# One pipeline of four phases over MoBA's eight heads, and two wide products first in keys and queries

## The chip, the cores and the metric

The kernel runs on one core of a Trainium2 chip. The metric is device microseconds of one execution. The changed kernel and the kernel before are timed on the same chip; differences under about 0.2% can't be told from none.

## The reference

One decoder layer on 256 tokens of width 1024, all in float32. A combined projection `x @ w_in` feeds two mixers: a gated linear recurrence (HGRN2) and a block attention (MoBA). With 256 tokens there is one block, so MoBA here is causal softmax attention over 8 heads of width 128, with rotary keys and queries. Both mixers are projected, gated, added and projected again, then come two layer norms and a SwiGLU network.

```python
proj = jnp.einsum('bsd,dn->bsn', x, w_in)
hq, hf, hi, hg, mq, mk, mv, gate_logits = jnp.split(proj, offsets, axis=-1)
y_a = rms_norm(hgrn2_mixer(...), ...) * jax.nn.silu(hg)
y_b = moba_attention(apply_rope(mq), apply_rope(mk), mv)
z_a = y_a @ w_branch_a; z_b = y_b @ w_branch_b
mixed = (g_a * z_a + g_b * z_b) @ w_out
x = layer_norm(DN_ALPHA * x + mixed, ln1_w, ln1_b)
y = (jax.nn.silu(h_gate) * h_up) @ w_ffn_down
return layer_norm(DN_ALPHA * x + y, ln2_w, ln2_b)
```

## The kernel before

Every large product is made of reduced-precision float32 (`fp32r`) parts: an operand is split into a high part (a cast on ScalarE, L192 or L220) and a low part (a subtraction on VectorE, L193 or L222), and TensorE adds high by high, high by low and low by high. The weights come as 77 tiles of 128 x 2048 in a fixed order (`plan`); `fetch` hands out the next pair `wh`, `wl` and keeps three more tiles being loaded, cast and subtracted ahead of it. There are three buffers for raw tiles and four for each of `wh` and `wl`, so a cast of tile i waits until TensorE has read tile i-4.

The change lies in the middle of the program. There the products with `w_in` for the attention are made: values `mv` (`values`, two halves of four heads), keys `mk` and queries `mq` (`rope_pair`, a pair of heads j each, j = 0 to 3), then the gate logits `ga` (`gates`), then the branch product `za`. `rope_pair` for j over 0 uses `wide_pair` (L324): for each k a product of 512 columns with `wh` (L335: x's high and low parts side by side) and one of 256 columns with `wl` (L337). Its argument `twos` says how many times, at the start of the tile's first half, two products with `wh` stand before two with `wl`.

Beside these products run the attention's heads (`moba_head`), as a generator that a list of side work (`Steps`) advances by one step after each `rope_pair` and after each half chunk of `values`, `gates` and `za`. A head has these parts:
- the split of its keys and queries into `kh`, `kl`, `qh`, `ql` on ScalarE and VectorE;
- the scores `s`: on TensorE one float32 product of 128 columns (L700, which the trace records as two matmuls) and three `fp32r` products (L705 to L707);
- the softmax in `ms` and `st`: VectorE adds the mask and takes maxima, ScalarE takes exponentials (L715, L716), VectorE scales by the reciprocals (L717 to L719);
- three transposes `pt` on TensorE (L723), copied out as `pTh`, `pTl` and `p1` (L727, L728);
- the product with the values, `po`, four matmuls (L731 to L734), split into `ybh`, `ybl`, which the branch product `zb` reads.

`moba_heads(h0, n)` runs four heads: a head's score part one step ahead of its transposes and its value product, which stand in the same step. Four heads are queued after keys and queries j = 1, the other four after j = 3, when the gate logits begin. ScalarE uses exponentials in the heads and sigmoids in the gate logits; to go from one to the other it loads a table (ACT_TABLE_LOAD).

The code's order gives only the dependences and a priority: in this part a scheduler sets each engine's order by its own timeline. Each engine then runs its list strictly in that order.

Of the kernel before, what the change touches and what calls it, by code (L numbers as in the profile page):

```python
# [11 lines left out]
F32R = mybir.dt.float32r  # L12
# [5 lines left out]
P = 128  # L18
T = 256
# [3 lines left out]
H = 8  # L23
# [15 lines left out]
HOLD_DOWN = 3  # L39
SUMS = 2  # L40
ORDERED = 2
DOWN = "SSPSTSTSPPP"
SUMS_AFTER = (8,12)
FAST = tuple(range(2, 2 + len(DOWN) - DOWN.count("P")))
PLAIN = tuple(q for q in range(NF // 2) if q not in FAST)
SEQUENCE = [PLAIN[DOWN[:i].count("P")] if s == "P" else FAST[i - DOWN[:i].count("P")] for i, s in enumerate(DOWN)]
AHEAD = [q for q, s in zip(SEQUENCE, DOWN) if s == "T"]

# [77 lines left out]
def hybrid_layer_kernel(ctx: ExitStack, tc, x, xw, vecs, bias, wts, ln1_w, ln1_b, ln2_w, ln2_b, consts, out):  # L126
# [7 lines left out]
    sm = pool("sm", 2)  # L134
    klp = pool("klp", 1)
    mm = pool("mm", 4, space=PSUM)
    aux = pool("aux", 4, space=PSUM)

    def slot(name, dt=F32):
        return big.tile([P, 2048], dt, tag="s8", name=name)  # L140

    def r32(ap):
        return ap.bitcast(F32)
# [47 lines left out]
    def split(dst_h, dst_l, src):  # L191
        nc.scalar.copy(dst_h, src)  # L192
        nc.vector.tensor_sub(dst_l, src, r32(dst_h))  # L193
# [84 lines left out]
    def fetch(ahead=LOOKAHEAD):  # L278
        while state["next"] < len(loads) and len(ready) < 1 + ahead:
            list(stage())  # L280
        return ready.pop(0)
# [6 lines left out]
    xp = Pair("xp")  # L288
# [27 lines left out]
    def feat_pair(name, ah=None, al=None):  # L316
        ah, al = (xTh, xTl) if ah is None else (ah, al)
        wh, wl = fetch()
        ps = mm.tile([P, 2, T], F32, tag="mm", name=name)
        for f in range(2):  # L320
            feat_steps(ps[:, f, :], wh, wl, f, ah, al, range(KC))
        return ps

    def wide_pair(name, a, p, tag, twos=0):  # L324


        wh, wl = fetch()
        pss = []
        for f in range(2):
            ps = p.tile([P, 2, T], F32, tag=tag, name=f"{name}{f}")  # L330
            wcol = slice(f * P, (f + 1) * P)
            n = twos if f == 0 else 0
            for ks in [(k, k + 1) for k in range(0, 2 * n, 2)] + [(k,) for k in range(2 * n, KC)]:
                for k in ks:
                    nc.tensor.matmul(ps, wh[:, k, wcol], a.both(k), start=(k == 0), stop=False)  # L335
                for k in ks:
                    nc.tensor.matmul(ps[:, 0, :], wl[:, k, wcol], a[0, k, slice(0, T)],  # L337
                                     start=False, stop=(k == KC - 1))
            pss.append(ps)
        return pss  # L340
# [114 lines left out]
    for j in range(4):  # L455
        sg = sm.tile([P, 2, T], F32, tag="sg", name=f"sgq{j}")
        sgs = [by_half(sg[:, f, :]) for f in range(2)]
        if j < HQ_WIDE:
            for f, ps in enumerate(wide_pair(f"hq{j}", xp, mm, "mm")):
                z = Qg[:, :, 2 * j + f, :]  # L460
# [7 lines left out]
        for f in range(2):  # L468
            h = 2 * j + f
# [156 lines left out]
    side = Steps()  # L626
# [17 lines left out]
    def values(c):  # L644
        cs = slice(c * 512, (c + 1) * 512)

        def evac(t, ps):
            if t == 0:
                split(mvh[:, cs], mvl[:, cs], ps)
            else:  # L650
                nc.scalar.copy(mv1[:, cs], ps)

        for _ in tok_chunk(f"mv{c}", evac):
            side.step()
# [21 lines left out]
    qT = slot("qT").rearrange("p (h t) -> p h t", h=H)  # L676
    kT = slot("kT").rearrange("p (h t) -> p h t", h=H)
# [3 lines left out]
    def rope_pair(nm, dst, j):  # L681
        if j == 0:
            ps = feat_pair(f"m{nm}{j}")
        else:
            ps = sm.tile([P, 2, T], F32, tag="sg", name=f"z{nm}{j}")
            for f, parts in enumerate(wide_pair(f"m{nm}{j}", xp, mm, "mm", {1: 1, 2: 2}.get(j, 0) if nm == "k" else 0)):
                nc.scalar.copy(ps[:, f, :], parts[:, 1, :])
                nc.vector.tensor_add(ps[:, f, :], parts[:, 0, :], ps[:, f, :])
        hs = slice(2 * j, 2 * j + 2)
        bc = lambda z: z[:, None, :].to_broadcast([P, 2, T])  # L690
        tmp = sm.tile([P, 2, T], F32, tag="sg", name=f"rt{nm}{j}")
        nc.scalar.copy(tmp[0:64], ps[64:P])
        nc.scalar.copy(tmp[64:P], ps[0:64])
        nc.vector.tensor_mul(dst[:, hs, :], ps, bc(cos))
        nc.gpsimd.tensor_mul(tmp, tmp, bc(sin))
        nc.gpsimd.tensor_add(dst[:, hs, :], dst[:, hs, :], tmp)

    def moba_head(h):
        ps = aux.tile([P, 3 * P], F32, tag="aux", name=f"s{h}")
        nc.tensor.matmul(ps[:, 0:P], qT[:, h, 0:P], kT[:, h, 0:P], start=True, stop=True)  # L700
        (kh, kl), (qh, ql) = [[sm.tile([P, n], F32R, tag=f"{tag}{z}", name=f"{nm}{z}{h}") for z in "hl"]
                              for nm, n, tag in (("k", T, "pT"), ("q", P, "q"))]
        split(kh, kl, kT[:, h, :])
        split(qh, ql, qT[:, h, P:T])
        nc.tensor.matmul(ps[:, P:3 * P], qh, kh, start=True, stop=False)  # L705
        nc.tensor.matmul(ps[:, P:3 * P], qh, kl, start=False, stop=False)
        nc.tensor.matmul(ps[:, P:3 * P], ql, kh, start=False, stop=True)  # L707
        s = sm.tile([P, 3 * P], F32, tag="ms", name=f"ms{h}")
        st = sm.tile([P, 8], F32, tag="st", name=f"st{h}")
        nc.vector.tensor_tensor(s, ps, causal, op=ALU.add)  # L710
        nc.vector.reduce_max(st[:, 0:1], s[:, 0:P], axis=mybir.AxisListType.X)
        nc.vector.reduce_max(st[:, 1:2], s[:, P:3 * P], axis=mybir.AxisListType.X)
        nc.vector.tensor_scalar(st[:, 2:4], st[:, 0:2], -SCALE, None, op0=ALU.mult)
        p = s
        nc.scalar.activation(p[:, 0:P], s[:, 0:P], AF.Exp, bias=st[:, 2:3], scale=SCALE, accum_out=st[:, 4:5])  # L715
        nc.scalar.activation(p[:, P:3 * P], s[:, P:3 * P], AF.Exp, bias=st[:, 3:4], scale=SCALE, accum_out=st[:, 5:6])  # L716
        nc.vector.reciprocal(st[:, 6:8], st[:, 4:6])  # L717
        nc.vector.tensor_scalar(p[:, 0:P], p[:, 0:P], st[:, 6:7], None, op0=ALU.mult)
        nc.vector.tensor_scalar(p[:, P:3 * P], p[:, P:3 * P], st[:, 7:8], None, op0=ALU.mult)  # L719
        yield  # L720
        pt = aux.tile([P, 3 * P], F32, tag="aux", name=f"pt{h}")
        for b in range(3):
            nc.tensor.transpose(pt[:, b * P:(b + 1) * P], p[:, b * P:(b + 1) * P], ident)  # L723
        pTh = sm.tile([P, T], F32R, tag="pTh", name=f"pTh{h}")
        pTl = sm.tile([P, T], F32R, tag="pTl", name=f"pTl{h}")
        p1 = sm.tile([P, P], F32, tag="pT", name=f"p1{h}")
        split(pTh, pTl, pt[:, 0:T])  # L727
        nc.scalar.copy(p1, pt[:, T:3 * P])  # L728
        hd = slice(h * P, (h + 1) * P)
        po = aux.tile([P, T], F32, tag="aux", name=f"po{h}")  # L730
        nc.tensor.matmul(po, mvh[:, hd], pTh, start=True, stop=False)  # L731
        nc.tensor.matmul(po, mvl[:, hd], pTh, start=False, stop=False)
        nc.tensor.matmul(po[:, P:T], mv1[:, hd], p1, start=False, stop=False)
        nc.tensor.matmul(po, mvh[:, hd], pTl, start=False, stop=True)  # L734
        split(ybh[:, h, :], ybl[:, h, :], po)
        yield

    def moba_heads(h0, n):
        heads = [moba_head(h) for h in range(h0, h0 + n)]
        next(heads[0])  # L740
        for i in range(n):
            if i < n - 1:
                next(heads[i + 1])
            next(heads[i])
            yield

    for c in range(2):
        if c == 1:
            values(1)
        for j in range(2 * c, 2 * c + 2):  # L750
            rope_pair("k", kT, j)
            side.step()
            rope_pair("q", qT, j)
            side.step()
        side.gens.append(moba_heads(4 * c, 4))
    ga = gates("ga", 0)


# [207 lines left out]

    for j in range(EARLY, NF - 2 * ORDERED, 2):
        ffn_step(j)

    with tc.manual_schedule(engines={ET.PE, ET.DVE, ET.Activation}):  # L970
        for j in range(NF - 2 * ORDERED, NF, 2):
            ffn_step(j)
# [54 lines left out]
        z, spare = [slot("z")[:, i:i + D] for i in (0, D)]  # L1027
# [8 lines left out]
        for i, (raw, (k0, wh, wl)) in enumerate(zip(last_raw, held)):  # L1036
# [5 lines left out]
            c = sums[:, 2 * i:2 * i + 2].unsqueeze(2).to_broadcast([P, 2, SUMS])  # L1042
# [106 lines left out]
```

## Time and profile before

| | |
|---|---|
| median of 3 runs | 492.94 us (492.85 to 493.57) |
| profiled execution: its time | 493.46 us |
| its span, first to last instruction | 491.7 us |
| mean granted TensorE clock | 0.998 |
| casts of weights on ScalarE (L220), 71 | 133.7 us busy, 1890 ns each |
| subtractions of weights on VectorE (L222), 71 | 162.4 us busy, 2293 ns each |

The span holds 1.8 us less than the time of the same execution. The page gives the busy time of each engine, the chain that ended last, and the groups of instructions; matmuls are pipelined, so one that is recorded with 389 ns lets the next start after some 230 ns. The distance between two starts is therefore what a matmul costs, and it is read from the timeline.

### The profile page before, as it was taken

The page shows a single profiled execution, that of the slowest core. Times are in us where ns is not written, and L with a number is a line of the kernel's source. Part 1 is how long each engine was busy: PE and PEld are TensorE (multiplying, and loading weights), DVE is VectorE, ACT ScalarE, POOL GpSimd, SP SyncE. Part 2 cuts the span into 40 slices and gives each one's busy share as a digit, 9 for nine tenths or more (in the row PEclk, how much of TensorE's full clock was granted, in tenths as well). Part 3 has the DMA queues.
Part 4 walks back from the last instruction along what each step waited for, and adds up shares of the span by engine and source line. Part 5 has one row for each costly group of instructions (what it writes and reads, how often), then busy time and mean ns, then how long its engine had stood idle before and what let it go on. Part 6 is the DMA issues. An engine that isn't in the chain of part 4 may idle for free.

```text
span 491.7 us, 6779 instructions
## 1 busy us (share of the span) xinstructions
PE 484.4 (99%) x2621; PEld 418.2 (85%) x2621; DVE 406.5 (83%) x523; ACT 297.5 (61%) x415; POOL 41.6 (8%) x46
## 2 busy tenths in 40 slices
PE   9999999999999999999999999999999999999994
PEld 9889888888899888888888888888888888888784
DVE  5879899999667998988765678856897878989996
ACT  6698587435756767777653462544655655576663
POOL 0000000000004441240000000000000000000030
PEclk9999999999999999999999999999999999999999
DMA  8977426644552346349544455247859644267852
GB/s 314 420 285 261 172 93 249 227 159 171 172 171 87 136 167 239 122 162 337 179 165 171 167 181 232 101 176 276 318 219 338 214 171 173 91 231 244 317 145 85
DMA packets 17631, 99.99 MB, mean 203 GB/s; under 512 B 1984, under 2 KB 3776, under 8 KB 7616
## 3 DMA queue, kind: packets, MB, share of 16 engines
q1 hardware_dynamic: 14400, 92.62, 51.9%
q0 software_dynamic: 3056, 6.82, 4.2%
q8 instruction: 20, 0.33, 0.3%
q10 hardware_dynamic: 144, 0.13, 0.1%
q14 instruction: 11, 0.09, 0.0%
HBM read 94.84 MB, written 3.15 MB: 199 GB/s over the span
## 4 chain that ended last, share of the span: by engine, by line
PE 90%; DVE 5%; issue 2%; ACT 1%; DMA 1%; DVEq 0%; POOLq 0%; POOL 0%; ACTq 0%
PE fu L335 7%; PE fg L335 7%; PE fg L337 3%; PE fu L337 3%; PE mk L335 2%; PE mq L335 2%; PE hq L335 2%; PE sc L542 2%; PE ga L387 1%; PE hf L360 1%; PE ga L388 1%; PE ga L386 1%; PE za L386 1%; PE za L387 1%; PE mv L386 1%
## 5 line engine op out<-in xcount | busy, mean ns | idle before, releaser
L222 DVE TENSOR_TENSOR wl<-raw,wh 128x2048 fp32r<-128x2048 f32 (+1 forms) x71 | 162.4, 2293 | 48.2 <-ACT wh L220 47.9
L220 ACT CAST wh<-raw 128x2048 fp32r<-128x2048 f32 (+1 forms) x71 | 133.7, 1890 | 62.2 <-PE fg L335 14.2
L335 PE MATMUL fg<-x1p,wh 128*128 128x512 f32 x144 | 50.5, 394 | 0.0
L335 PE MATMUL fu<-x1p,wh 128*128 128x512 f32 x144 | 50.4, 394 | 0.0
L337 PE MATMUL fg<-x1p,wl 128*128 128x256 f32 x144 | 40.0, 278 | 0.0
L337 PE MATMUL fu<-x1p,wl 128*128 128x256 f32 x144 | 39.9, 277 | 0.0
L335 PEld LDWEIGHTS fu<-x1p,wh 128*128 128x128 f32 x144 | 27.0, 187 | 6.2
L335 PEld LDWEIGHTS fg<-x1p,wh 128*128 128x128 f32 x144 | 27.0, 187 | 6.1
L337 PEld LDWEIGHTS fg<-x1p,wl 128*128 128x128 f32 x144 | 27.1, 188 | 0.1
L337 PEld LDWEIGHTS fu<-x1p,wl 128*128 128x128 f32 x144 | 27.1, 188 | 0.0
L335 PE MATMUL mq<-xp,wh 128*128 128x512 f32 x48 | 17.2, 396 | 0.0
L335 PE MATMUL mk<-xp,wh 128*128 128x512 f32 x48 | 17.0, 397 | 0.0
L589 POOL TENSOR_TENSOR ost<-ost,half 128x4 f32<-128x4 f32 x4 | 4.1, 1015 | 152.7 <-DVE ost L588 152.7
L335 PE MATMUL hq<-xp,wh 128*128 128x512 f32 x48 | 16.7, 394 | 0.0
L337 PE MATMUL mq<-xp,wl 128*128 128x256 f32 x48 | 13.5, 282 | 0.0
L337 PE MATMUL hq<-xp,wl 128*128 128x256 f32 x48 | 13.3, 277 | 0.0
L337 PE MATMUL mk<-xp,wl 128*128 128x256 f32 x48 | 13.1, 284 | 0.0
L388 PE MATMUL ga<-wl,xp 128*128 128x512 f32 x32 | 12.7, 398 | 0.0
L387 PE MATMUL za<-wh,yal 128*128 128x512 f32 x32 | 12.7, 397 | 0.0
L879 PE MATMUL fe<-wh,x1p 128*128 128x512 f32 x32 | 12.6, 395 | 0.0
L388 PE MATMUL gb<-wl,xp 128*128 128x512 f32 x32 | 12.6, 395 | 0.0
L805 PE MATMUL wo<-wh,mTh 128*128 128x512 f32 x32 | 12.6, 394 | 0.0
(379 smaller groups left out, 1367.9 us busy)
## 6 DMA issues: line engine op xcount, KB each, us to landing
raw<-in_wts_dram SPq DMA_DIRECT2D x69, 1024.0 KB, 4.8
rawcorners<-in_wts_dram SPq DMA_DIRECT2D x5, 1024.0 KB, 4.8
xw<-in_xw_dram SPq DMA_DIRECT2D x6, 640.0 KB, 8.8
rawahead<-in_wts_dram SPq DMA_DIRECT2D x2, 1024.0 KB, 4.9
rawsums<-spill SPq DMA_DIRECT2D x2, 1024.0 KB, 4.8
rawcorners<-in_wts_dram SPq DMA_DIRECT2D x2, 768.0 KB, 5.9
raw<-in_wts_dram SPq DMA_DIRECT2D x2, 512.0 KB, 11.8
xr<-in_x_dram POOLq DMA_DIRECT2D x1, 1024.0 KB, 5.4
```

The lines of the kernel that those rows point to most:

```text
L220: nc.scalar.copy(h[:, ks, :], raw[:, ks, :])
L222: eng.tensor_sub(l[:, ks, :], raw[:, ks, :], r32(h[:, ks, :]))
L335: nc.tensor.matmul(ps, wh[:, k, wcol], a.both(k), start=(k == 0), stop=False)
L337: nc.tensor.matmul(ps[:, 0, :], wl[:, k, wcol], a[0, k, slice(0, T)], start=False, stop=(k == KC - 1))
L360: nc.tensor.matmul(ps, wh[:, kk, wcol], xp.both(k), start=False, stop=False)
L386: nc.tensor.matmul(pss[t], ah[:, kk, ts], wh[:, k, :], start=(kk == 0), stop=False)
L387: nc.tensor.matmul(pss[t], al[:, kk, ts], wh[:, k, :], start=False, stop=False)
L388: nc.tensor.matmul(pss[t], ah[:, kk, ts], wl[:, k, :], start=False, stop=(kk == KC - 1))
L542: nc.tensor.matmul(ps[:, a, :], KL[:, h, :], later(Qt, n, h, 1), start=True, stop=True)
L589: nc.gpsimd.tensor_tensor(st[:, 8:12], st[:, 4:8], half, op=ALU.pow)
L805: nc.tensor.matmul(ps, lh(kk)[:, ts], wh[:, k, ns], start=(kk == first), stop=False)
L879: nc.tensor.matmul(ps, x1p[0, kk, ts], wh[:, k, :], start=(kk == 0), stop=False)
```

## The change

Four things are changed.

1. All eight heads form one pipeline, queued once, after keys and queries j = 1. A head begins at a step of its own (`STARTS`: 0, 1, 3, 5, 6, 7, 8, 9).
2. A head has four phases, at `LAGS` 0, 1, 3 and 5 steps after its beginning: the split of keys and queries; scores and softmax; transposes and their copies; the value product. In one step, older phases come first. The pipeline has 15 steps.
3. Keys' high and low parts lie in one tile `keys` of four slices (two heads), in the buffer that the recurrence used before, instead of two buffers each that they shared with the transposes' copies.
4. `twos` is 1 for all wide keys and for queries j = 2 and 3. Before it was 1 and 2 for keys j = 1 and 2 and 0 elsewhere.

```diff
+STARTS = (0, 1, 3, 5, 6, 7, 8, 9)
+LAGS = (0, 1, 3, 5)
...
-            for f, parts in enumerate(wide_pair(f"m{nm}{j}", xp, mm, "mm", {1: 1, 2: 2}.get(j, 0) if nm == "k" else 0)):
+            for f, parts in enumerate(wide_pair(f"m{nm}{j}", xp, mm, "mm", int(nm == "k" or j > 1))):
...
-    def moba_head(h):
+    def moba_head(h, keys):
+        kh, kl = [keys[:, 2 * (h % 2) + z, :] for z in range(2)]
+        qh, ql = [sm.tile([P, P], F32R, tag=f"q{z}", name=f"q{z}{h}") for z in "hl"]
+        split(kh, kl, kT[:, h, :])
+        split(qh, ql, qT[:, h, P:T])
+        yield
         ps = aux.tile([P, 3 * P], F32, tag="aux", name=f"s{h}")
         nc.tensor.matmul(ps[:, 0:P], qT[:, h, 0:P], kT[:, h, 0:P], start=True, stop=True)
-        (kh, kl), (qh, ql) = [[sm.tile([P, n], F32R, tag=f"{tag}{z}", name=f"{nm}{z}{h}") for z in "hl"]
-                              for nm, n, tag in (("k", T, "pT"), ("q", P, "q"))]
-        split(kh, kl, kT[:, h, :])
-        split(qh, ql, qT[:, h, P:T])
...
         nc.scalar.copy(p1, pt[:, T:3 * P])
+        yield
...
-    def moba_heads(h0, n):
-        heads = [moba_head(h) for h in range(h0, h0 + n)]
-        next(heads[0])
-        for i in range(n):
-            if i < n - 1:
-                next(heads[i + 1])
-            next(heads[i])
+    def moba_heads():
+        keys = klp.tile([P, 4, T], F32R, tag="kl", name="keys")
+        heads = [moba_head(h, keys) for h in range(H)]
+        for i in range(STARTS[-1] + LAGS[-1] + 1):
+            for lag in LAGS[::-1]:
+                for head, start in zip(heads, STARTS):
+                    if i == start + lag:
+                        next(head, None)
             yield
...
-        side.gens.append(moba_heads(4 * c, 4))
+        if c == 0:
+            side.gens.append(moba_heads())
```

What the scheduler makes of it is seen at three places. In these rows the changed kernel's line numbers are a few higher (L707 to L710 are the score products, L726 the transposes, L735 to L738 the value products), and the number behind a name's letters is the head.

On TensorE, in the first quarter of the branch product `za`, before:

```order
L731 MATMUL po4_2090<-pTh4_2084,mv_958 128x256
L732 MATMUL po4_2090<-pTh4_2084,mv_958 128x256
L700 MATMUL s6_2131<-kT_1319,qT_1318 128x128
L705 MATMUL s6_2131<-kh6_2133,qh6_2135 128x256
L723 MATMUL pt5_2155<-cst_89,ms5_2069 128x128
L706 MATMUL s6_2131<-kl6_2134,qh6_2135 128x256
L707 MATMUL s6_2131<-kh6_2133,ql6_2136 128x256
L723 MATMUL pt5_2155<-cst_89,ms5_2069 128x128 x2
```

and now:

```order
L726 MATMUL pt5_2207<-cst_89,ms5_2117 128x128 x3
L707 MATMUL s7_2217<-kT_1319,qT_1318 128x128
L708 MATMUL s7_2217<-keys_1596,qh7_2194 128x256
L709 MATMUL s7_2217<-keys_1596,qh7_2194 128x256
L710 MATMUL s7_2217<-keys_1596,ql7_2195 128x256
L735 MATMUL po4_2265<-pTh4_2172,mv_958 128x256
L736 MATMUL po4_2265<-pTh4_2172,mv_958 128x256
L737 MATMUL po4_2265<-p14_2174,mv1_959 128x128
L738 MATMUL po4_2265<-pTl4_2173,mv_958 128x256
L726 MATMUL pt6_2272<-cst_89,ms6_2183 128x128 x3
```

Parts of heads that lay among each other, with products of `za` between, are now whole and stand in a row; in the whole program the groups of float32 products of 128 columns on TensorE go from 51 to 43, with the same number of products in them. Between the transposes `pt4` and the transposes `pt5` there stand now the scores `s6`, the value product `po3` and 38 products of `za`.

On ScalarE, at the same time, before (`ga` rows are sigmoids, `ms` rows exponentials):

```order
L715 ACT_TABLE_LOAD
L715 ACTIVATE ms4_2045,st4_2046<-ms4_2045,st4_2046 128x128
L716 ACTIVATE ms4_2045,st4_2046<-ms4_2045,st4_2046 128x256
L220 CAST wh34_2246<-raw34_2245 128x2048
L715 ACTIVATE ms5_2069,st5_2070<-ms5_2069,st5_2070 128x128
L716 ACTIVATE ms5_2069,st5_2070<-ms5_2069,st5_2070 128x256
L667 ACT_TABLE_LOAD
L667 ACTIVATE ga_1999<-ga_1999 128x512
L192 CAST pTh4_2084<-pt4_2080 128x256
L192 CAST kh6_2133<-kT_1319 128x256
L220 CAST wh35_2299<-raw35_2298 128x2048
L667 ACTIVATE ga_1999<-ga_1999 128x512
```

and now, from the row behind the cast `wh35`:

```order
L669 ACT_TABLE_LOAD
L669 ACTIVATE ga_1935<-ga_1935 128x512
L718 ACT_TABLE_LOAD
L718 ACTIVATE ms5_2117,st5_2118<-ms5_2117,st5_2118 128x128
L719 ACTIVATE ms5_2117,st5_2118<-ms5_2117,st5_2118 128x256
L194 CAST pTh4_2172<-pt4_2168 128x256
L669 ACT_TABLE_LOAD
L669 ACTIVATE ga_1935<-ga_1935 128x512
L194 CAST ybh_1320<-po3_2200 128x256
L718 ACT_TABLE_LOAD
L718 ACTIVATE ms6_2183,st6_2184<-ms6_2183,st6_2184 128x128
L719 ACTIVATE ms6_2183,st6_2184<-ms6_2183,st6_2184 128x256
```

The two sigmoids of the last gate chunk stood together and now have the exponentials of head 5 between them: the program has two table loads more. The row behind the last one shown is the copy `p14` that `po4` above reads.

On ScalarE, while the queries j = 3 are made, now (`zk3` rows take keys j = 3 from PSUM, `rtq2` rows are the rotary halves of queries j = 2):

```order
L222 CAST wh30_1871<-raw30_1870 128x2048
L694 COPY rtq2_1770<-zq2_1725 64x512
L695 COPY rtq2_1770<-zq2_1725 64x512
L194 CAST pTh1_1847<-pt1_1843 128x256
L194 CAST keys_1596<-kT_1319 128x256
L194 CAST ybh_1320<-po0_1920 128x256
L689 COPY zk3_1792<-mk30_1799 128x256
L689 COPY zk3_1792<-mk31_1816 128x256
L718 ACTIVATE ms2_1858,st2_1859<-ms2_1858,st2_1859 128x128
L719 ACTIVATE ms2_1858,st2_1859<-ms2_1858,st2_1859 128x256
L731 COPY p11_1849<-pt1_1843 128x128
```

Before, the copy `p11` of head 1 came well ahead of the exponentials of head 2 (five rows ahead, with the weight cast `wh29` between them); now it stands behind them. The orders of SyncE, and of all engines before the values' second half and behind the first products of `zb`, are unchanged; on GpSimd one transfer has moved ahead of one rotary sum.

## The prediction

> **What bounds the kernel now.** I read the page first: busy time, clock, and the chain that ended last.
>
> ```profile
> span 491.7 us, 6779 instructions
> ...
> PE 484.4 (99%) x2621; PEld 418.2 (85%) x2621; DVE 406.5 (83%) x523; ACT 297.5 (61%) x415; POOL 41.6 (8%) x46
> ...
> PEclk9999999999999999999999999999999999999999
> ...
> PE 90%; DVE 5%; issue 2%; ACT 1%; DMA 1%; DVEq 0%; POOLq 0%; POOL 0%; ACTq 0%
> ```
>
> TensorE (PE) is busy for 484.4 of 491.7 us at full clock, and the chain runs 90% on it. A busy TensorE may still have idled between pipelined matmuls, so the second view is its waits, the whole list for that engine:
>
> ```profile
> PE warm L429 <- PEq L1136: 0.8, 1, 0.8
> ```
>
> It waits once, at the start. The third view is busy time by stretch (columns: length, then busy time and count for PE, weight loads, DVE, ACT, POOL), over the queries and keys, the gate logits, and the branch product `za`:
>
> ```profile
> 182.40:208.00 25.60, 25.60 (x158) 22.67 (x157) 21.93 (x44) 19.79 (x45) 6.83 (x6) 1.00 0.53 188
> 208.00:233.00 25.00, 25.00 (x124) 20.91 (x123) 21.02 (x35) 19.59 (x33) 7.18 (x7) 1.00 0.66 249
> 233.00:259.00 26.00, 26.00 (x133) 21.94 (x132) 18.45 (x32) 15.50 (x29) 0.00 (x0) 1.00 0.51 173
> ```
>
> TensorE fills every stretch that the change touches, while ScalarE has 5 to 10 us free in each. So this part ends when TensorE's list of matmuls ends. A new order gains only if the same matmuls cost less in it; it loses as soon as one of them comes due before its input is there.
>
> **The change, part by part.** *Gathered parts of heads.* No matmul is added or taken away; the float32 products of 128 columns lie in 43 groups instead of 51. What is a group's cost? Starts from the timeline, first three transposes in a row, then three that are parted by a product:
>
> ```profile
> 186.47 0.49 PE L723 MATMUL pt<-cst,ms 128*128 128x128 f32 x3
> 186.71 0.37 PE L337 MATMUL mk<-xp,wl 128*128 128x256 f32 x1
> 186.92 0.39 PE L335 MATMUL mk<-xp,wh 128*128 128x512 f32 x1
> ...
> 250.16 0.27 PE L723 MATMUL pt<-cst,ms 128*128 128x128 f32 x1
> 250.19 0.48 PE L386 MATMUL za<-wh,yah 128*128 128x512 f32 x1
> 250.50 0.38 PE L723 MATMUL pt<-cst,ms 128*128 128x128 f32 x2
> 250.64 0.48 PE L387 MATMUL za<-wh,yal 128*128 128x512 f32 x1
> 250.95 0.39 PE L388 MATMUL za<-wl,yah 128*128 128x512 f32 x1
> ```
>
> In a row: 186.47 to 186.92 is 0.45 us, less 0.12 for one 256-column product, 0.33. Parted: 250.16 to 250.95 is 0.79, less two 512-column products of 0.23, again 0.33. Each transpose costs 0.11 in either order. (The product behind a group seems 0.09 slow only because the group's starts are drawn together.) The score part agrees:
>
> ```profile
> 173.05 0.38 PE L700 MATMUL s<-kT,qT 128*128 128x128 f32 x2
> 173.18 0.37 PE L705 MATMUL s<-kh,qh 128*128 128x256 f32 x1
> 173.38 0.39 PE L386 MATMUL mv<-wh,xp 128*128 128x512 f32 x1
> ```
>
> 0.33 is two records of 0.11 and one product of 0.12. So gathering is worth 0.0 us. Bounds: if each group did cost 0.09 once, 8 fewer would gain 0.7; at the other end, nothing. I take 0, by the parted group, which is the direct comparison.
>
> *Two wide products first.* Keys j = 2 begins in that order, then alternates:
>
> ```profile
> 182.42 0.62 PE L335 MATMUL mk<-xp,wh 128*128 128x512 f32 x2
> ...
> 183.80 0.40 PE L335 MATMUL mk<-xp,wh 128*128 128x512 f32 x1
> ...
> 184.50 0.40 PE L335 MATMUL mk<-xp,wh 128*128 128x512 f32 x1
> ```
>
> Four pairs in 1.38 us, 0.345 each; two alternating pairs in 0.70, 0.35 each. The doubled beginnings go from 3 to 5: below 0.02 us. They give a late `wl` 0.23 us more, but TensorE never waited for one. 0.0.
>
> *ScalarE and VectorE.* Two table loads are added, the rest is moved. Here a cost appears only where TensorE is made to wait, so I work out the places where a matmul now stands soonest behind its input. The rows (for ScalarE then VectorE):
>
> ```profile
> 219.52 0.64 ACT L667 ACTIVATE ga<-ga 128x512 f32<-128x512 f32 x1
> 225.64 1.28 ACT L715 ACT_TABLE_LOAD   x1
> 226.93 0.40 ACT L715 ACTIVATE ms<-ms,st 128x128 f32<-128x128 f32 x1
> 227.73 0.19 ACT L716 ACTIVATION_READ_ACCUMULATOR ms<-ms,st 128x1 f32 x1
> 227.83 1.89 ACT L220 CAST wh<-raw 128x2048 fp32r<-128x2048 f32 x1
> 233.28 0.35 ACT L192 CAST pTh<-pt 128x256 fp32r<-128x256 f32 x1
> 241.81 0.26 ACT L728 COPY p<-pt 128x128 f32<-128x128 f32 x1
> ...
> 227.95 0.17 DVE L717 RECIPROCAL st<-st 128x2 f32<-128x2 f32 x1 [0.91 <-ACT ms L716]
> 228.35 0.35 DVE L719 TENSOR_SCALAR ms<-ms,st 128x256 f32<-128x256 f32 x1
> 229.75 2.29 DVE L222 TENSOR_TENSOR wl<-raw,wh 128x2048 fp32r<-128x2048 f32 x1 [1.05 <-ACT wh L220]
> 243.89 0.42 DVE L193 TENSOR_TENSOR ybl<-po,ybh 128x256 fp32r<-128x256 f32 x1
> ```
>
> A table load holds ScalarE for 1.29, a head's two exponentials for 0.90, reciprocal and scaling take 0.75. Two loads more are 2.6 us of ScalarE, covered by its idle time, unless a chain through them is due.
>
> Place A, first quarter of `za`. Let 0 be the end of the last `ga` product. TensorE: `pt4` 0.33, `s6` 0.57 (0.22 and three of 0.12), 38 products of `za` 8.76, `po3` 0.57, so it reaches `pt5` at 10.2, after that and `s7` and two products of `po4` the copy `p14` at 11.4, and `pt6` at 11.7. ScalarE: `wh35` may begin at 0, when `wh31` has been read: 1.91, load 1.29, sigmoid 0.65, load 1.29, exponentials 0.90 (done 6.1), `pTh4` 0.37, load 1.29, sigmoid 0.54, `ybh` of head 3 0.38 (8.6), load 1.29, exponentials 0.90 (10.9), `p14` 0.26: 11.1. VectorE scales head 5 behind the `ybl` that waits for that `ybh`: 8.6 + 0.42 + 0.6 = 9.6, against 10.2. `p14`: 11.1 against 11.4. Head 6: 10.9 + 0.75 = 11.65, against 11.7. Spare: 0.6, 0.3, 0.1.
>
> Place B, queries j = 3. Here GpSimd comes in. In this profile its rotary product stood still while VectorE subtracted, and then VectorE's two 128 x 2 scalings took 1.33 while GpSimd worked:
>
> ```profile
> 179.44 3.13 POOL L695 TENSOR_TENSOR rtq<-rtq,cst 128x512 f32<-128x512 f32 x1 [5.73 <-ACT rtq L693]
> ...
> 179.14 2.28 DVE L222 TENSOR_TENSOR wl<-raw,wh 128x2048 fp32r<-128x2048 f32 x1
> 181.34 1.33 DVE L713 TENSOR_SCALAR st<-st 128x2 f32<-128x2 f32 x2
> ```
>
> Let 0 be the start of `s2`. TensorE reaches the read of `p11` at 0.57 + 0.57 + 16 x 0.348 + 0.23 = 6.9. `wh30` ends at 1.8, its `wl` at 4.1; the rotary product then runs to 5.4, head 2's scaling behind it to 5.5, its exponentials to 6.4, and `p11` behind those to 6.7. Spare 0.2. Without the collision it is 1.3 more.
>
> The chains have a dozen links that I know to some 0.03 us each, so a spare of 0.1 to 0.3 may be a wait of as much: I cost each place at 0.0, with 0.5 as its upper end. All other new waits have over 1 us by the same count: head h + 2 overwrites its slice of `keys` over 1 us behind the scores of head h. On GpSimd, the issue of one transfer now stands ahead of the rotary sum of queries j = 3:
>
> ```profile
> 218.60 0.92 POOL L836 DMA_DIRECT2D xr<-in_x_dram  x1
> ```
>
> That sum comes 0.9 later. Its first reader is the query cast of head 6, whose scores come some 12 us later on TensorE, so ScalarE may wait there a little and TensorE doesn't. Weights stay three tiles ahead, so no `wh` or `wl` is late; behind a wait on TensorE stands only its own list, and everything later shifts with it.
>
> One rule of the Trainium skill speaks against the change. "ScalarE: Activation LUTs", section "What ACT_TABLE_LOAD costs", gives about 2.66 us for every switch, a load of 1283 ns and a drain of 1380. The row above has the 1.28 and no drain: the exponential starts 0.01 behind the load. By the page's price place A, with four loads, would be 5.5 us later.
>
> **The sum.** 0.0 + 0.0 + 0.0 on a span of 491.7, or 493.46 for the profiled execution. That lies 0.5 over the median of the runs, 492.94, to which the same sum applies: **493.0 us**.
>
> **The rivals.**
> - *Gathering pays* (0.07): each group costs 0.09 on the way back to wide products, as the drawn rows suggest. 493.0 - 0.7 = 492.3; to be over 0.2% (1 us) it needs a gain elsewhere too, 0.04 of it.
> - *Small waits* (0.10): the spares at A and B are used up; two waits of 0.3 to 0.5 give 493.6 to 493.9.
> - *Place A decides, slower* (0.14): `p14` and `pt6` follow a chain of four loads on one engine. If anything ahead of it on ScalarE, the `wh35` cast or the wait of the second load for VectorE, is late by x, TensorE waits for x less the 0.1 to 0.3 spare. From x = 1.3 it is over 0.2%. With 1.5 to 2, 494.2 to 494.8. Against it: `wh35` waits only for products that are over, and ScalarE has nothing else due then.
> - *A switch costs twice its row* (0.02): the engine empties first, for as long again as the load's 1.28. Four loads, 5.1 less the 0.3 spare: 497.8. Against it stands the row of the next exponential, 0.01 behind the load. It is the kind of cost that the skill's page above describes.
> - *Forecast, nothing moves* (0.67): 492.6 to 493.4.
>
> About 0.2%, 1.0 us, is what a measurement of this kernel can tell from no change. Faster 0.04; within, 0.67 + 0.10 + 0.03 = 0.80; slower 0.14 + 0.02 = 0.16. The range takes in the full price of gathering below and waits of up to 1.5 us above: 492.2 to 494.5; some 0.1 is left out, nearly all above.
>
> **What would show it.** TensorE's waits should again hold only the start's 0.8. The gathered parts should cost 0.11 for each 128-column record. ScalarE should show two loads of 1.28 more, with the next instruction 0.01 behind. If place A decides, TensorE shows gaps ahead of `pt5`, the float32 product of `po4` or `pt6`; if B, ahead of that of `po1`. The forecast is wrong if TensorE's list takes less time with no wait gone, since then matmuls have costs that these rows don't show.

## The result, and the profile after

The changed kernel is slower: 496.79 us median of 6 runs (496.29 to 497.73), against 493.12 for the kernel before on the same chip; ratio 1.0075, 95% interval 1.0062 to 1.0088, so about 3.7 us. Its profiled execution took 496.85 us with a span of 494.8, at nearly the same granted clock (0.996, before 0.998). The spans differ by 3.1. Another 0.3 lies outside the span (time less span is 2.05, before 1.76), and the profiled execution of before lay 0.34 above its median: together the 3.7.

The page of the changed kernel, the lines that answer to those shown of before:

```profile
span 494.8 us, 6780 instructions
...
PE 485.7 (98%) x2621; PEld 418.7 (85%) x2621; DVE 408.0 (82%) x523; ACT 299.3 (60%) x417; POOL 41.6 (8%) x46
...
PEclk9999999999999999999999999999999999999998
...
PE 74%; DVE 12%; ACT 7%; issue 4%; DMA 1%; DVEq 0%; POOLq 0%; POOL 0%; ACTq 0%
```

The list of matmuls is as long as before (x2621), but the chain that ended last now runs only 74% on TensorE instead of 90%, and through VectorE and ScalarE instead. TensorE's waits name the places:

```profile
PE pt L726 <- DVE ms L721: 1.3, 1, 1.3
PE warm L431 <- PEq L1142: 0.8, 1, 0.8
PE ga L388 <- DVE zk L690: 0.6, 1, 0.6
PE po L737 <- ACT p L731: 0.3, 1, 0.3
```

(The columns behind the names are the total in us, the number of waits and the longest.) Two of the three new ones (`pt`, `po`) are place A of the prediction. The list shows less than the places cost: starts of matmuls, below, give 2.55 at A where it has 1.3 and 0.3. The third, `ga`, is at place B's end, but not the wait that the prediction counted there. The same stretches as before:

```profile
182.40:208.00 25.60, 25.01 (x153) 22.04 (x152) 23.06 (x40) 18.12 (x39) 6.21 (x4) 1.00 0.61 217
208.00:233.00 25.00, 24.98 (x123) 21.01 (x124) 20.47 (x36) 18.97 (x33) 8.28 (x7) 1.00 0.60 206
233.00:259.00 26.00, 24.44 (x121) 19.84 (x120) 19.40 (x39) 19.02 (x32) 0.00 (x0) 1.00 0.40 140
```

TensorE was busy in all of each stretch before; now 0.6 is missing in the first and 1.6 in the third, where ScalarE has gone from 15.50 to 19.02 of 26.

**Place A, followed back.** The prediction began its count with the cast `wh35` at 0, the end of `ga`. TensorE's rows there (`pt4` at 232.98 is that end; the next is `pt5`, then `po4`'s float32 product, then `pt6`):

```profile
232.98 0.49 PE L726 MATMUL pt<-cst,ms 128*128 128x128 f32 x3
...
244.91 0.70 PE L726 MATMUL pt<-cst,ms 128*128 128x128 f32 x3 [1.26 <-DVE ms L721]
...
246.71 0.49 PE L737 MATMUL po<-p,mv 128*128 128x128 f32 x2 [0.28 <-ACT p L731]
...
247.16 0.63 PE L726 MATMUL pt<-cst,ms 128*128 128x128 f32 x3
```

And ScalarE's timeline: the exponential of head 3, then, some twenty rows on, the copy `p13`, the cast `wh35` and the loads behind it:

```profile
221.58 0.41 ACT L718 ACTIVATE ms<-ms,st 128x128 f32<-128x128 f32 x1 [3.90 <-DVE st L716]
...
235.44 0.27 ACT L731 COPY p<-pt 128x128 f32<-128x128 f32 x1 [2.51 <-DVE pTl L195]
235.60 1.92 ACT L222 CAST wh<-raw 128x2048 fp32r<-128x2048 f32 x1
237.54 1.28 ACT L669 ACT_TABLE_LOAD   x1
238.83 0.63 ACT L669 ACTIVATE ga<-ga 128x512 f32<-128x512 f32 x1
239.47 1.28 ACT L718 ACT_TABLE_LOAD   x1
```

`wh35` begins at 235.60, which is 2.6 behind the end of `ga`, not 0. Ahead of it in ScalarE's list stands `p13`, which has nothing to do with `wh35`: it simply comes first, and waited 2.51 for VectorE's split `pTl`. (That wait alone isn't the lateness: in the run below in which `wh35` is on time, `p13` waits 2.50 as well. What counts is how late the rows ahead of it come.) From there on every row is as the prediction counted it: cast, load, sigmoid, load, without a gap.

Why was VectorE late? VectorE's timeline at three places (scaling of head 3; `wl34` and `pTl3`; the end of the chain), then GpSimd's:

```profile
217.20 3.17 DVE L224 TENSOR_TENSOR wl<-raw,wh 128x2048 fp32r<-128x2048 f32 x1
220.29 1.25 DVE L716 TENSOR_SCALAR st<-st 128x2 f32<-128x2 f32 x1
...
231.93 2.29 DVE L224 TENSOR_TENSOR wl<-raw,wh 128x2048 fp32r<-128x2048 f32 x1 [0.58 <-ACT wh L222]
...
234.99 0.42 DVE L195 TENSOR_TENSOR pTl<-pt,pTh 128x256 fp32r<-128x256 f32 x1
...
244.24 0.42 DVE L195 TENSOR_TENSOR ybl<-po,ybh 128x256 fp32r<-128x256 f32 x1 [1.78 <-ACT ybh L194]
244.58 0.28 DVE L721 TENSOR_SCALAR ms<-ms,st 128x128 f32<-128x128 f32 x1
```

```profile
216.92 1.29 POOL L697 TENSOR_TENSOR rtq<-rtq,cst 128x512 f32<-128x512 f32 x1 [4.63 <-ACT rtq L695]
218.17 0.92 POOL L842 DMA_DIRECT2D xr<-in_x_dram  x1
219.11 2.41 POOL L698 TENSOR_TENSOR qT<-qT,rtq 128x512 f32<-128x512 f32 x1
```

Read from the top: GpSimd's rotary product (216.92 to 218.21) holds up the subtraction for `wl32`, 3.17 instead of 2.28; the subtraction holds up GpSimd's sum (2.41 instead of 1.29); the sum holds up the scaling of two numbers per row (1.25 instead of 0.16). The transfer that the change put ahead of the sum is not what makes the sum late: it ends at 219.09, while the subtraction runs until 220.37. Head 3's exponential waits 3.9 for that scaling (1.97 of it remain when the two GpSimd operations are made small, below), and with it everything that stands behind it on ScalarE: a cast, a subtraction that waits for the cast, a head's step that stands behind the subtraction, the next cast. So the delay goes round between the two queues from 221 to 235, through casts and small steps that wait for one another in list order. It starts 14 us and three tiles ahead of `wh35`, and TensorE feels it at `pt5`, 23 us behind.

The collision itself is not new. The kernel before has such collisions too (1.33 for two scalings in the prediction's row at 181.34; 1.26 for one at 203.37), and TensorE waits for nothing there. What is new is which steps meet and what stands behind them: with queries j = 3 it held up only a weight's subtraction there, by 0.4 (2.72 from 218.08), and no head's scaling.

**Place B.** VectorE's rows, then GpSimd's, ahead of the first product of `ga` at 208.02:

```profile
204.32 1.26 DVE L716 TENSOR_SCALAR st<-st 128x2 f32<-128x2 f32 x1
205.49 0.41 DVE L195 TENSOR_TENSOR pTl<-pt,pTh 128x256 fp32r<-128x256 f32 x1
205.82 1.38 DVE L195 TENSOR_TENSOR keys<-kT,keys 128x256 fp32r<-128x256 f32 x1
...
207.46 0.74 DVE L690 TENSOR_TENSOR zk<-mk,zk 128x256 f32<-128x256 f32 x2
```

```profile
203.22 2.33 POOL L697 TENSOR_TENSOR rtq<-rtq,cst 128x512 f32<-128x512 f32 x1 [6.01 <-ACT rtq L695]
205.63 1.29 POOL L698 TENSOR_TENSOR qT<-qT,rtq 128x512 f32<-128x512 f32 x1
```

The two additions `zk` empty the PSUM banks of keys j = 3, and `ga`'s first product needs one of those banks. They stand behind two steps that GpSimd holds up by some 1.1 and 1.0 us (the usual lengths are 0.16 and 0.41). TensorE waits 0.6 by the profile; the distances between starts below give 0.8.

### The profile page after: what moved, and what is told of

Read it like the earlier page. It is cut to its first block, busy times and chain, and to the rows that moved or that the text cites. A ratio compares the mean times of both kernels' runs of the same rounds, so it can differ in the third digit from the quotient of the medians.

```text
span 494.8 us, 6780 instructions
## 1 busy us (share of the span) xinstructions
PE 485.7 (98%) x2621; PEld 418.7 (85%) x2621; DVE 408.0 (82%) x523; ACT 299.3 (60%) x417; POOL 41.6 (8%) x46
## 4 chain that ended last, share of the span: by engine, by line
PE 74%; DVE 12%; ACT 7%; issue 4%; DMA 1%; DVEq 0%; POOLq 0%; POOL 0%; ACTq 0%
PE fu L337 7%; PE fg L337 7%; DVE wl L224 5%; ACT wh L222 3%; PE fg L339 3%; PE fu L339 3%; PE hq L337 2%; PE sc L544 2%; PE hf L362 1%; PE zb L389 1%; PE zb L388 1%; PE gb L388 1%; PE fe L885 1%; PE fe L887 1%; PE wo L813 1%
## 5 line engine op out<-in xcount | busy, mean ns | idle before, releaser
L224 DVE TENSOR_TENSOR wl<-raw,wh 128x2048 fp32r<-128x2048 f32 (+1 forms) x71 | 164.2, 2318 | 48.9 <-ACT wh L222 48.5
L388 PE MATMUL ga<-wh,xp 128*128 128x512 f32 x32 | 12.6, 393 | 0.6 <-DVE zk L690 0.6
L388 PE MATMUL zb<-wh,ybh 128*128 128x512 f32 x32 | 12.6, 393 | 0.0
```

Source lines behind the costliest of these rows:

```text
L224: eng.tensor_sub(l[:, ks, :], raw[:, ks, :], r32(h[:, ks, :]))
L388: nc.tensor.matmul(pss[t], ah[:, kk, ts], wh[:, k, :], start=(kk == 0), stop=False)
```

## The experiments

Theory: ScalarE's and VectorE's lists, run strictly in order, reach places A and B late; at A it takes both the lateness and the loads between sigmoids and exponentials. Rivals: the loads alone; the lateness alone; the new `twos`; the gathered parts on TensorE itself; any order as dense as this. Each ratio is to the kernel before on the same chip; the experiments ran on other chips than the result, so across paragraphs the ratios compare, not the medians.

**Which part of the change?** The kernel before with only the twos, and the changed kernel without them:

```diff
-            ... "mm", {1: 1, 2: 2}.get(j, 0) if nm == "k" else 0)):
+            ... "mm", int(nm == "k" or j > 1))):
```

> The kernel before with only the two 512-column products at the beginning of keys j = 0 to 3 and queries j = 2, 3 as the change has them; the heads stay two groups of two phases. Queues of the other engines are unchanged. My theory (the waits at places A and B, which come from the heads' order): nothing, 493.1 within 0.3, TensorE waits 0.8 at the start alone. Rival (the doubled beginnings cost on TensorE themselves): a part of the 3.7 us shows here, at least 493.7.

> The changed kernel with the twos of before: only the heads' new pipeline is left. My theory: all of the 3.7 us, 496.5 to 497.0, with TensorE's waits of 1.3 for ms and 0.6 for zk as in the changed kernel. Rival (the doubled beginnings cost, or they shift TensorE into the waits): under 496.

Twos alone: 493.3 us, ratio 0.9998 (0.9990 to 1.0007): nothing. Heads alone: 497.99, ratio 1.0090 (1.0076 to 1.0105), the same three waits of 1.3, 0.6 and 0.3. Its median is 1.0 above the expected range. In its profiled execution the excess lies ahead of the change: the first `hq` product starts at 29.26, in the changed kernel at 27.81, and from there to TensorE's last matmul it takes 460.62 against 460.55. One of its five executions took 496.09, the others some 498. Why the start took longer there is open. From keys to `wo` this kernel takes 146.83, the whole change 146.76 (table below): there the cost of the heads is that of the whole change.

**Are the table loads in it?** The sigmoid of `ga` becomes an exponential, in the changed kernel and, as a control, in the kernel before:

```diff
-                nc.scalar.activation(g[:, t, cs], g[:, t, cs], AF.Sigmoid)
+                nc.scalar.activation(g[:, t, cs], g[:, t, cs], AF.Exp if name == "ga" else AF.Sigmoid)
```

> The changed kernel with the sigmoid of the gate ga replaced by an exponential, so that ScalarE needs 6 table loads instead of 12; the sigmoid of that gate is left out. All queues have the same order as in the changed kernel. My theory, ScalarE's chain at place A (third phase of heads 4 to 6 in the first quarter of za) with the four loads in it: the waits at pt5 and ahead of po4 (some 2.2 us together) are gone, the one ahead of the first ga product (0.6 to 0.8, behind VectorE) stays or shrinks a little: 494.0 to 494.7. Rival 1 (the chain is late for VectorE's sake alone, by wh35's late start, and the loads are only beside it): 496 or more. Rival 2 (the gathered parts cost on TensorE itself): 496.8.

> The same replacement in the kernel before (6 table loads instead of 10; the sigmoid of that gate is left out), as a control. All theories but one: TensorE waits for no load there, so 493.1 within 0.3. If a load costs time of its own wherever it stands: about 5 us less, 488.

493.74 us, ratio 1.0013 (1.0005 to 1.0022), and 493.05 for the control, 1.0000 (0.9991 to 1.0009). TensorE's waits without the loads, in the changed kernel:

```profile
PE warm L431 <- PEq L1142: 0.8, 1, 0.8
PE ga L388 <- DVE zk L690: 0.6, 1, 0.6
PE hf L359 <- ACT fh L194: 0.6, 1, 0.6
```

The waits for `ms` and `p` are gone, the one for `zk` stays, and the time is 0.3 below the range that I gave. (The wait of `hf`, near the program's start, comes and goes between executions: the twos alone show 0.5, the changed kernel none.) Yet here `wh35` was late too:

```profile
234.36 1.91 ACT L222 CAST wh<-raw 128x2048 fp32r<-128x2048 f32 x1
236.16 0.63 ACT L669 ACTIVATE ga<-ga 128x512 f32<-128x512 f32 x1
```

234.36 is 1.42 behind that kernel's `pt4` (232.94). So 1.42 of lateness without the loads costs nothing at A, and in the kernel before four loads less gain nothing. The loads are in the lateness too: without them it is 1.42 and not 2.62. Two of the six that are gone stood ahead of `wh35` (at 222.74 and 227.50 in the changed kernel). The full 2.62 without loads behind it was not measured.

**Does the lateness come from GpSimd?** Its two rotary operations work on 16 columns per row instead of all, for queries j = 3, for j = 2, and for both:

```diff
-        nc.gpsimd.tensor_mul(tmp, tmp, bc(sin))
-        nc.gpsimd.tensor_add(dst[:, hs, :], dst[:, hs, :], tmp)
+        w = 16 if nm == "q" and j > 1 else T
+        nc.gpsimd.tensor_mul(tmp[:, :, 0:w], tmp[:, :, 0:w], sin[:, None, 0:w].to_broadcast([P, 2, w]))
+        nc.gpsimd.tensor_add(dst[:, hs, 0:w], dst[:, hs, 0:w], tmp[:, :, 0:w])
```

> The changed kernel in which GpSimd's two rotary operations for queries j = 3 work on 16 columns of each row instead of all: the rotation of heads 6 and 7's other columns is left out. All other queues keep their order. Without the collision the wl subtraction takes 2.3 instead of 3.2 and the scaling of head 3 some 0.15 instead of 1.25, so that its exponential, which now waits 3.9, comes 1.9 earlier. My theory (at place A the loads decide only because wh35 begins 2.6 late, and that comes from this collision by way of heads 3, 4 and wl33, wl34): wh35 begins 1.5 to 1.9 earlier, the waits at pt5 and p14 fall from 2.2 to 0.3 or 0.5, the one ahead of ga stays: 494.7 to 495.3. Rival (the four loads are too much for place A wherever wh35 begins, or wh35 is late for another reason): 496.5 to 497.

> The changed kernel in which GpSimd's two rotary operations for queries j = 2 work on 16 columns of each row (the rotation of heads 4 and 5's other columns is left out); a few instructions of TensorE and ScalarE change places. Theory for the wait ahead of the first ga product: zk3 on VectorE stands behind a scaling and a split that GpSimd holds up by 1.1 us each, so without them TensorE doesn't wait there, and place A stays: 495.8 to 496.2. Rival (GpSimd is beside the matter, VectorE is late by its own list): 496.6 to 497.

> The changed kernel with its sigmoid and all 12 table loads, and GpSimd's rotary operations for queries j = 2 and 3 on 16 columns of each row (the rotation of heads 4 to 7's other columns is left out). Runs so far had wh35 begin 2.6, 1.2 and 0.7 behind the end of ga, and TensorE waits in za of about that less 0.1 to 0.3. My theory (the prediction's sum for place A was right, its input was wrong: the wait is what wh35 is late, less 0.3): without either collision wh35 begins 0.3 early to 0.5 late, TensorE waits 0 to 0.3 in za, 492.8 to 493.3. Rival (four loads there cost TensorE some 0.5 or more even with wh35 on time): 493.5 to 494.3.

j = 3: 494.61 us, ratio 1.0029 (1.0017 to 1.0040), just under what was expected. j = 2: 494.32, 1.0035 (1.0021 to 1.0048), with three of 11 executions above 495.7; the median is 1.5 under the expected range. B's wait is gone as expected, but so is more than half of A's, which I had not expected. The trace shows how: VectorE comes earlier, so that its subtraction for `wl32` now begins ahead of GpSimd's product for j = 3 and isn't held up (2.28 instead of 3.17):

```profile
215.39 2.28 DVE L224 TENSOR_TENSOR wl<-raw,wh 128x2048 fp32r<-128x2048 f32 x1
...
216.14 2.69 POOL L698 TENSOR_TENSOR rtq<-rtq,cst 128x512 f32<-128x512 f32 x1 [5.64 <-ACT rtq L695]
```

Head 3's exponential waits 2.00 there instead of 3.90. Both: 493.00, 0.9996 (0.9987 to 1.0005), as expected. In that last one all 12 loads are there, `wh35` starts at 231.46 and `pt4` at 231.49, and TensorE waits for no head:

```profile
230.99 0.27 ACT L731 COPY p<-pt 128x128 f32<-128x128 f32 x1 [2.50 <-DVE pTl L195]
231.46 1.91 ACT L222 CAST wh<-raw 128x2048 fp32r<-128x2048 f32 x1 [0.21 <-PE ga L389]
233.39 1.28 ACT L669 ACT_TABLE_LOAD   x1
```

```profile
231.49 0.49 PE L726 MATMUL pt<-cst,ms 128*128 128x128 f32 x3
...
241.63 0.49 PE L726 MATMUL pt<-cst,ms 128*128 128x128 f32 x3
...
243.12 0.52 PE L726 MATMUL pt<-cst,ms 128*128 128x128 f32 x3
```

Between the starts of `pt4` and `pt6` TensorE has the same matmuls in all these kernels, so that distance measures A's wait:

| kernel | `wh35` behind `pt4` | `pt4` to `pt6` | wait over the last row |
|---|---|---|---|
| changed | 2.62 | 14.18 | 2.55 |
| j = 2 small | 1.18 | 12.73 | 1.10 |
| j = 3 small | 0.73 | 12.28 | 0.65 |
| both small | -0.03 | 11.63 | 0 |
| no switches | 1.42 | 11.67 | 0.04 |

With the loads, TensorE waits what `wh35` is late, less 0.1. Without them, 1.42 late costs nothing. One limit: with small j = 2 operations a few instructions of TensorE, ScalarE and VectorE also change places ahead of A. The runs without switches and with small j = 3 operations keep these engines' orders (on GpSimd the transfer goes back behind the sum), and they alone already show the loads and the collision at A.

**Both causes out.** What is the order itself worth?

> The changed kernel with both causes taken out: ga's sigmoid replaced by an exponential (6 table loads; the sigmoid of that gate is left out), and GpSimd's rotary operations for queries j = 2 and 3 on 16 columns of each row (the rotation of heads 4 to 7's other columns is left out). TensorE then has no wait in the stretches that the change touches, so the time says what the gathered parts and the twos are worth on TensorE by themselves, against 493.1. My prediction's price, 0.0: 492.8 to 493.4. Rival (a group costs some 0.05 to 0.09 on TensorE, so gathering pays, and the waits hid it): 492.4 to 492.7. Rival (the new parts cost on TensorE): over 493.5.

492.85 us, ratio 0.9990 (0.9981 to 0.9998), within the range for a price of 0.0. The starts of the first products of keys, `ga` and `wo` tell where; in the kernel before:

```profile
138.76 0.28 PE L346 MATMUL mk<-xp,wh 128*128 128x256 f32 x1
...
208.08 0.40 PE L386 MATMUL ga<-wh,xp 128*128 128x512 f32 x1
...
282.23 0.39 PE L805 MATMUL wo<-wh,mTh 128*128 128x512 f32 x1
```

| kernel | keys to `ga` | `ga` to `wo` | together |
|---|---|---|---|
| before | 69.32 | 74.15 | 143.47 |
| twos alone | 69.36 | 74.18 | 143.54 |
| changed | 69.21 | 77.55 | 146.76 |
| no switches | 69.20 | 74.92 | 144.12 |
| both small, with loads | 68.38 | 74.81 | 143.19 |
| both causes out | 68.38 | 74.78 | 143.16 |
| heads alone | 69.23 | 77.60 | 146.83 |
| no scaling (below) | 68.39 | 74.82 | 143.21 |

(Before and after have other parts of heads ahead of `ga`, so between those two only the sum compares.) Place B costs 69.21 - 68.38 = 0.83, place A with its neighbourhood 77.55 - 74.81 = 2.74. The three changed kernels that don't wait are 0.26 to 0.31 below before, each in one profiled execution; the three kernels with the heads as before (before, twos alone, and before without switches) lie between 143.46 and 143.54.

**Other ways to mend it.** Heads 4 to 7 begin behind the last sigmoid; then heads 2 and 3 also at other steps; then no scaling `st` at all, in the changed kernel and in the one before:

```diff
-STARTS = (0, 1, 3, 5, 6, 7, 8, 9)
+STARTS = (0, 1, 3, 5, 9, 10, 11, 12)
...
+STARTS = (0, 1, 3, 4, 9, 10, 11, 12)
```

```diff
-        nc.vector.tensor_tensor(s, ps, causal, op=ALU.add)
-        nc.vector.reduce_max(st[:, 0:1], s[:, 0:P], axis=mybir.AxisListType.X)
-        nc.vector.tensor_scalar(st[:, 2:4], st[:, 0:2], -SCALE, None, op0=ALU.mult)
+        nc.vector.scalar_tensor_tensor(s, ps, -SCALE, causal, op0=ALU.mult, op1=ALU.subtract)
+        nc.vector.tensor_reduce(st[:, 2:3], s[:, 0:P], axis=mybir.AxisListType.X, op=ALU.min)
...
-        nc.scalar.activation(p[:, 0:P], s[:, 0:P], AF.Exp, bias=st[:, 2:3], scale=SCALE, accum_out=st[:, 4:5])
+        nc.scalar.activation(p[:, 0:P], s[:, 0:P], AF.Exp, bias=st[:, 2:3], scale=-1.0, accum_out=st[:, 4:5])
```

> The changed kernel with STARTS (0, 1, 3, 5, 9, 10, 11, 12), so that heads 4 to 7 begin after the last sigmoid of ga: 8 table loads instead of 12, and none between exponentials in za. The same is computed. Theory of the loads: the waits in za are gone, the one of 0.6 to 0.8 ahead of ga stays: 493.6 to 494.2. Rival (head chains of this density make TensorE wait in za or zb also without loads): above 495, with new waits for ms, p or ybh.

> As the kernel with heads 4 to 7 later, and with heads 2 and 3 at steps 3 and 4 instead of 3 and 5: head 3's scores come ahead of ga, and head 2's float32 product and pt3 into ga. The same is computed, with 8 table loads. Theory: the ga wait behind VectorE depends on which head step stands ahead of zk3 there; if it goes, 492.9 to 493.4, as before; if it stays, 493.6 to 494.2. Rival (fewer loads than before and gathered parts pay on TensorE): under 492.5.

> The changed kernel without the scaling st: the scores are multiplied by -SCALE as the causal mask is subtracted, the smallest is the exponential's bias as it is. The same is computed, with one VectorE operation per head less. The order is planned anew by itself: 10 table loads, ga's last two sigmoids together in za, so two loads between sigmoids and exponentials there instead of four. Theory: the waits in za fall to 0.5 or less, and the exponential no longer stands behind the small scaling; ahead of ga VectorE's zk3 is less late: 493.1 to 494.2. Rival (any density of heads like this one makes TensorE wait): 495 or more.

> The kernel before without the scaling st, as a control. The same is computed. TensorE waits for no head there, so nothing: 493.1 within 0.3. If heads' small operations on VectorE cost TensorE time in a way that its waits don't show: 492.7 or less.

Heads 4 to 7 later: 494.80 us, ratio 1.0035 (1.0022 to 1.0047), 0.6 above the expected range. The waits in `za` are gone and the one ahead of `ga` is still there, as expected, but there is a new one, which the second version has as well (494.07, 1.0021, 1.0012 to 1.0030, 0.7 above what was expected if the wait ahead of `ga` went, and it did go):

```profile
PE mt L778 <- DVE ga L787: 0.6, 1, 0.6
```

TensorE's transposes of the merged branches now come too soon behind the product that VectorE has to merge first. The expectation missed that the order behind `za` moves as well; why the scheduler puts them there was not followed further.

No scaling: 493.03 us, 0.9993 (0.9984 to 1.0001), with no wait for a head. This computes the same as the changed kernel in 0.8% less (ratios 0.9993 and 1.0075), and can't be told from the kernel before. It changes more than one thing (10 loads, two sigmoids of `ga` side by side, another order), so it shows that the pipeline can be had without loss, not which of these mends it. The control is 493.74, 1.0008 (1.0000 to 1.0016): at the edge of what can be told, 0.3 above the range expected. In its profiled execution it takes 69.82 from keys to `ga` and 143.90 from keys to `wo`, 0.4 more than before, with no wait listed in that stretch; which of its moved steps costs that was not followed. Nothing is gained.

## Why the prediction was wrong

- *TensorE's list sets the end, so only new waits can cost.* Right. With the waits removed the change is at 492.85 to 493.03 (ratios 0.9990 to 0.9996), as forecast.
- *Gathered parts, 0.0, bounds 0 and 0.7.* Within the bounds, the size perhaps a little off: 0.26 to 0.31 in the profiled executions. If all of it belonged to the 8 groups, it would be 0.04 each, but no run changes the groups alone, and the rows around single groups still give 0.11 for a record (the three transposes `pt4` of the changed kernel run from 232.98 to 233.30). In medians the three versions without waits gain 0.04% to 0.10%, two of three intervals holding 1.
- *Twos, 0.0.* Right, 0.9998 (0.9990 to 1.0007).
- *Place A's sum.* Its arithmetic held: four loads, spare 0.1 at `pt6`; the tables above give 0.1. **The step that failed is its first input**: "`wh35` may begin at 0, when `wh31` has been read", and among the rivals "`wh35` waits only for products that are over, and ScalarE has nothing else due then". I looked at the wait for the buffer and not at the instruction ahead in ScalarE's list, `p13`, nor at what `p13` stands behind. The runs showed 2.62 in place of that 0; without the collisions it is -0.03, and even then ScalarE was free only 0.21 before the buffer was. With the x of 2.62 put into the rival "Place A decides, slower", the wait is 2.5, which is what was measured. The rival had the mechanism right; its x of 1.5 to 2 was too low.
- *Place B.* For `p11` TensorE waits in no row, as counted with the collision. But "All other new waits have over 1 us by the same count" was wrong: the wait of `ga`'s first product for the PSUM bank that `zk` frees was not on my list, though it stands behind the same two held-up steps. It costs 0.83.
- *"A switch costs twice its row".* Wrong: in the rows at A each load takes 1.28, starts 0.01 to 0.02 behind the row ahead of it, and the next row starts 0.01 behind it (235.60 + 1.92, 237.54 + 1.28, then 238.83), and with all 12 loads and no lateness the ratio is 0.9996. The Trainium skill's page "ScalarE: Activation LUTs", section "What ACT_TABLE_LOAD costs", has a drain of 1380 ns beside the load; these rows don't show one.
- *The collision of GpSimd and VectorE.* I priced it at B as a delay of 1.3 and did not carry it on. Queries j = 3 have the same collision, and A's lateness comes through it: small operations for j = 3 take it from 2.62 to 0.73, small ones for j = 2, which shift that collision, to 1.18. "ScalarE may wait there a little and TensorE doesn't" was said of the sum for j = 3, of its reader alone. What waited was head 3's exponential, 3.9 instead of 1.97, behind the scaling that the sum held up, and TensorE paid 23 us later.

The sum, in the profiled executions: A 2.74 and B 0.83, less the 0.28 by which the kernel that doesn't wait is below before, is 3.3, between keys and `wo` (146.76 - 143.47 = 3.29). The three terms are differences of the same tables, so they must add up; that A and B are what they stand for rests on the experiments.

## What to carry to other kernels

When engines run in list order, the input of a count ("this cast may begin at 0") needs the instruction ahead of it on its engine followed back until one is found that waits for nothing late; here the cause ended 14 us earlier, on an engine that is busy 8% of the time. In this kernel the full engine hid its helpers' costs only while they had slack: 1.4 us late without loads was free, four loads without lateness were free, and with both on one chain TensorE waited for nearly all of the lateness. Whoever moves small steps of one engine between long ones should also list each PSUM bank that they free late.

## What the runs showed of the hardware

Where a VectorE and a GpSimd instruction collide in these traces, they don't slow each other in proportion: the second stands still until the first is through, however small it is. In the kernel with small j = 3 operations, GpSimd's sum of 128 x 32 took 2.33, where the product of the same size took 0.25, beside a subtraction that ran from 217.34 to 219.62:

```profile
217.06 0.25 POOL L698 TENSOR_TENSOR rtq<-rtq,cst 128x32 f32<-128x32 f32 x1 [4.63 <-ACT rtq L695]
217.40 2.33 POOL L698 TENSOR_TENSOR qT<-qT,rtq 128x32 f32<-128x32 f32 x1
```

The Trainium skill's page "SBUF — State Buffer", section "Who interferes with whom", calls the port pair that the two share an exclusive lock. It names two kinds of VectorE instruction that contend for it with GpSimd: those with two inputs in SBUF, and those in a 2-port mode, where whoever issues first has the pair for its whole instruction and the other fully blocks. The subtractions `wl` and `keys` have two inputs in SBUF, and these rows agree, both ways round. Whether the 128 x 2 scaling runs in a 2-port mode no trace here says; that it is held up, 1.25 instead of 0.16, they do. Not every pair collides: at place B the split `pTl`, which reads one of its inputs from PSUM, took its usual 0.41 from 205.49 while GpSimd's sum ran from 205.63 in its usual 1.29. The surprise is how far a collision carries: the two operations for queries j = 3 take 3.7 us of GpSimd in the changed kernel, and with small ones in their place the ratio falls from 1.0075 to 1.0029, some 2.3 us.
